# A one-core decoder layer: merge, second norm and down projection in other slots, and the low parts of the input projection's weights kept in DRAM between the halves

## The chip, the cores and the metric

The kernel runs on one core of a Trainium2 chip. The metric is the device time of one execution in microseconds, the median of several runs; lower is better.

## The reference

One layer of a hybrid decoder for a prompt of 1024 tokens and 8 decoding samples of one token each, with D = 1024. All arithmetic is fp32. Cut to what matters:

```python
h = _rms_norm(x, norm_mix_g)
proj = h @ w_in                                   # 1024 x 5888: 46 blocks of 128 columns
p_rwkv, p_hgrn, p_gate = split(proj)              # 14, 16 and 16 blocks
o_a = _rwkv7_mixer(p_rwkv, ...)                   # delta-rule matrix state, 8 heads of 64
o_b = _hgrn2_mixer(p_hgrn, ...)                   # gated linear recurrence, 4 heads of 128
gate_a, gate_b = split(sigmoid(p_gate))
merged = gate_a * (o_a @ w_up_a) + gate_b * (o_b @ w_up_b)
x = x + merged @ w_out                            # output projection
h = _rms_norm(x, norm_ffn_g)                      # the second norm
x = x + (silu(h @ w_ffn_gate) * (h @ w_ffn_up)) @ w_ffn_down
y = _rms_norm(x, norm_final_g)
```

The new states of both mixers, for the prompt and the samples, are outputs too.

## The kernel before

The tokens are worked in two halves, 512 tokens and then 512 tokens with the 8 samples (520 columns, in two chunks of 260). Activations lie transposed: channels on the 128 partitions, tokens along the columns. A half goes through these stages: input projection and mixers, merge (`push_merge`), output projection (`push_out`). The feed-forward network and the down projection then take both halves together.

Every product runs three times on TensorE, since operands are split: a high part (a copy rounded to the fast fp32r type) and a low part (the difference). `wload` does this for a weight block of 128 x 1024: SP loads the raw tile `w`, ACT copies it to `wh`, and GpSimd (POOL) subtracts, in four pieces, to make `wl`. Each of the three tags has two buffers. `mm3` then gives TensorE per block of 128 rows the products wh x high, wh x low and wl x high: 24 matmuls of 512 columns for a weight in the first half, 48 of 260 in the second.

Work is recorded by two streams. `parts` holds generators (norms, preparations and chains of the mixers); `stream` and `fillers` hold dense weights (`push`, `fill`). `drive` advances the part that is due by the recorder's own clock and puts a step of dense work (`dense_step`) wherever no part is due; when a weight is begun, the next one is loaded (`preload`). A scheduler then sets the final order on each engine, and each engine runs its queue in order. Nearly all DMAs are issued by SP, whose queue is in order as well: a DMA that waits holds all that stand behind it. The fillers are the gates' weights.

In the RWKV mixer (`rwkv_prep`) each of four pairs of heads inverts triangular blocks through bursts of small DMAs to DRAM and back (d1, nb, na, d2, t32, ubd, ebd, tbd); `rwkv_chain` is a chain of small matmuls, DVE and ACT steps.

Slots are fixed tiles by tag (h 16, t 6, p 11, w 19, d 4 of double width, a 2 of triple width; n and s in the second part). After the second half's merge the kernel splits all eight merged tiles in one go (in `push_out`, into slots of w, d and a), and the second norm of the first half (`first_second_norm`: a sum of squares, `rstd`, `spread`, and in `second_norm` the scaled tiles, their differences and splits for a fast product scheme, stored in `h2t[0]`) is driven while the merge's weights run:

```python
    start("norm", first_second_norm())
    drive()
    finish_stream()
    ...
    h2t[1] = push_out(1, merged, x1, residual)
```

After the output projection come two blocks of the feed-forward network for the first half alone (`push_plain`), beside which the second half's second norm runs, then the network in the fast scheme, then the down projection in four groups of acts (`gslots`, `load_acts`, `push_down`).

## Time and profile before

| | us |
|---|---|
| median of 3 runs | 1928.99 |
| lowest of the runs | 1925.67 |
| the profiled execution | 1921.57 |
| its span, first to last instruction | 1919.8 |
| PE busy | 1772.6 (92%) |
| DVE, POOL, ACT busy | 1078.6, 969.0, 808.7 |

The profiled execution is one run with the hardware profiler; its span leaves out 1.8 us around the first and last instruction. Its mean granted TensorE clock was 0.963 of full speed. Busy PE is not PE at its peak: at the lower clock the same matmul is busy for longer.

### The profile page before, as it was taken

The page shows a single profiled execution, that of the slowest core. Times are in us where ns is not written, and L with a number is a line of the kernel's source. Part 1 is how long each engine was busy: PE and PEld are TensorE (multiplying, and loading weights), DVE is VectorE, ACT ScalarE, POOL GpSimd, SP SyncE. Part 2 cuts the span into 40 slices and gives each one's busy share as a digit, 9 for nine tenths or more (in the row PEclk, how much of TensorE's full clock was granted, in tenths as well). Part 3 has the DMA queues.
Part 4 walks back from the last instruction along what each step waited for, and adds up shares of the span by engine and source line. Part 5 has one row for each costly group of instructions (what it writes and reads, how often), then busy time and mean ns, then how long its engine had stood idle before and what let it go on. Part 6 is the DMA issues. An engine that isn't in the chain of part 4 may idle for free. (4 is left out here: it accounts for less than half of the span.)

```text
span 1919.8 us, 32939 instructions
## 1 busy us (share of the span) xinstructions
PE 1772.6 (92%) x12376; PEld 1628.9 (85%) x12376; DVE 1078.6 (56%) x2315; ACT 808.7 (42%) x1601; POOL 969.0 (50%) x1131
## 2 busy tenths in 40 slices
PE   6998999988799799899889869999999999999997
PEld 5776778778678789788889769999999999889987
DVE  4476577657465366567554593856656665531214
ACT  4446556656342456354344453433333333421111
POOL 6545555645365456556364364654434343542342
PEclk9998999999899899889989889999999999999998
DMA  4233233343444225323434543123221322732212
GB/s 133 87 72 98 84 81 84 113 131 112 150 161 126 76 66 88 103 70 95 124 114 129 175 156 130 67 89 105 72 84 67 103 75 95 253 109 56 72 52 89
DMA packets 172304, 199.05 MB, mean 104 GB/s; under 512 B 99632, under 2 KB 108080, under 8 KB 172144
## 3 DMA queue, kind: packets, MB, share of 16 engines
q1 hardware_dynamic: 172144, 196.94, 34.3%
q8 instruction: 97, 1.59, 0.4%
q14 instruction: 63, 0.52, 0.1%
HBM read 156.30 MB, written 40.07 MB: 102 GB/s over the span
## 5 line engine op out<-in xcount | busy, mean ns | idle before, releaser
L160 ACT ACT_TABLE_LOAD x66 | 84.7, 1283 | 1.8 <-PEq L1825 0.7
L160 POOL TENSOR_TENSOR d__20102<-d__20102,d__20103 128x512 f32<-128x512 f32 (+1 forms) x14 | 14.2, 1016 | 21.3 <-ACT d__20103 L160 21.3
L160 DVE SCALAR_TENSOR_TENSOR w__6304<-p__6021,vec,pm__6305 128x512 f32<-128x512 f32 x1 | 0.7, 747 | 21.2 <-PE pm__6305 L238 21.2
L238 PE MATMUL pd__12144<-w__12090,wh__12128 128*128 128x260 f32 x1 | 0.6, 584 | 13.0 <-ACT w__12090 L160 13.0
L160 POOL TENSOR_TENSOR wl__1389<-w__1386,wh__1388 128x256 fp32r<-128x256 f32 x4 | 3.2, 841 | 17.0 <-ACT wh__1388 L160 17.0
L160 POOL COPY own<-wkv_st 64x64 f32<-64x64 f32 x16 | 6.2, 386 | 10.7 <-PE pm__4635 L238 3.3
L238 PEld LDWEIGHTS pd__12144<-w__12090,wh__12128 128*128 128x128 f32 x1 | 0.3, 288 | 13.2 <-ACT w__12090 L160 13.2
L160 POOL TENSOR_TENSOR wl__11476<-w__11473,wh__11475 128x256 fp32r<-128x256 f32 x4 | 3.7, 940 | 14.3 <-ACT wh__11475 L160 14.3
L238 PE MATMUL pm__219<-ones,t__196 128*128 128x1 f32 x4 | 1.0, 357 | 9.5 <-DVE t__196 L160 9.5
L160 POOL TENSOR_TENSOR wl__5125<-w__5122,wh__5124 128x256 fp32r<-128x256 f32 x4 | 3.6, 936 | 11.3 <-ACT wh__5124 L160 11.3
L160 POOL TENSOR_TENSOR wl__10054<-w__10051,wh__10053 128x256 fp32r<-128x256 f32 x4 | 2.8, 736 | 12.7 <-ACT wh__10053 L160 12.7
L160 POOL TENSOR_TENSOR wl__3944<-w__3941,wh__3943 128x256 fp32r<-128x256 f32 x4 | 3.3, 855 | 11.8 <-ACT wh__3943 L160 11.8
L238 PEld LDWEIGHTS pm__219<-ones,t__196 128*128 128x128 f32 x4 | 0.9, 322 | 9.5 <-DVE t__196 L160 9.5
L160 POOL TENSOR_TENSOR wl__12202<-w__12199,wh__12201 128x256 fp32r<-128x256 f32 x4 | 2.8, 734 | 11.2 <-ACT wh__12201 L160 11.2
L238 PE MATMUL pm__6333<-t__6313,ebd 128*128 128x128 f32 x8 | 2.1, 441 | 6.6 <-ACT t__6313 L160 6.6
L238 PEld LDWEIGHTS pm__6333<-t__6313,ebd 128*128 128x128 f32 x8 | 1.8, 328 | 6.8 <-ACT t__6313 L160 6.8
L238 PE MATMUL pm__5093<-w__4985,wh__5071 128*128 128x512 f32 x1 | 0.8, 792 | 7.3 <-ACT w__4985 L160 7.3
L160 POOL TENSOR_TENSOR wl__10209<-w__10206,wh__10208 128x256 fp32r<-128x256 f32 x4 | 2.8, 733 | 8.7 <-ACT wh__10208 L160 8.7
L160 POOL TENSOR_TENSOR wl__6274<-w__6271,wh__6273 128x256 fp32r<-128x256 f32 x4 | 2.8, 719 | 8.7 <-ACT wh__6273 L160 8.7
L160 POOL TENSOR_TENSOR wl__1106<-w__1103,wh__1105 128x256 fp32r<-128x256 f32 x4 | 5.1, 1291 | 4.0 <-ACT wh__1105 L160 4.0
L160 POOL TENSOR_TENSOR wl__11397<-w__11394,wh__11396 128x256 fp32r<-128x256 f32 x4 | 2.8, 732 | 7.9 <-ACT wh__11396 L160 7.9
L238 PE MATMUL pc__7693<-vsz__7629,kbt__7700 128*128 128x128 f32 x2 | 0.8, 500 | 6.4 <-ACT vsz__7629 L160 6.4
(23703 smaller groups left out, 8520.1 us busy)
## 6 DMA issues: line engine op xcount, KB each, us to landing
tbd<-t SPq DMA_DIRECT2D x32, 32.0 KB
w__166<-in_w_in SPq DMA_DIRECT2D x1, 512.0 KB
w__184<-in_w_in SPq DMA_DIRECT2D x1, 512.0 KB
w__452<-in_w_in SPq DMA_DIRECT2D x1, 512.0 KB
w__461<-in_w_in SPq DMA_DIRECT2D x1, 512.0 KB
w__501<-in_w_in SPq DMA_DIRECT2D x1, 512.0 KB
w__541<-in_w_in SPq DMA_DIRECT2D x1, 512.0 KB
w__581<-in_w_in SPq DMA_DIRECT2D x1, 512.0 KB
```

Of the source, the lines that this page charges most:

```text
L160: return f(*args, **kw)
L238: PE.matmul(out, lhsT, rhs, start=start, stop=stop)
```

## The change

Two things are changed.

First, in the first half each input-projection weight, when it begins, has its low part stored to DRAM (`store_low`, 44 blocks of 512 KB). The two blocks of the low-rank parts, worked at the very start, are not stored, so POOL subtracts for them in both halves. In the second half `wload_in` loads the raw block and the stored low part by two DMAs, ACT makes the high part, and POOL does nothing for it. Five of the second half's 46 input weights run at the end of the first half's mixers, ahead of the first merge; two of these are the low-rank ones.

Second, the second half's merged tiles are split one by one as each is done (`done` of `push_merge`), into the h slots; the second norm of the first half keeps its sum of squares beside the merge, but its scaling, differences and splits are driven beside the output projection and go to slots of w, d and a. The acts of the down projection take their slots in another order of tags.

```diff
@@ -255,7 +255,23 @@
     V.memset(ones, 1.0)
 
 
-    def wload(src, k=KD, dst=None):
+
+    lows, stores = {}, {}
+
+    def wload_in(m, half):
+        if half == 0:
+            w = wload(i["w_in"][m])
+            stores[id(w)] = m
+            return w
+        return wload(i["w_in"][m], low=lows.get(m))
+
+    def store_low(w):
+        m = stores.pop(id(w), None)
+        if m is not None:
+            lows[m] = dp.tile([P, KD, P], F32, tag="low", name=nm("low"), bufs=NIN)
+            SP.dma_start(out=lows[m], in_=w[1].bitcast(F32))
+
+    def wload(src, k=KD, dst=None, low=None):
         w = wp.tile([P, KD, P], F32, tag="w", name=nm("w"))[:, :k]
         SP.dma_start(out=w, in_=src)
         if dst is None:
@@ -263,7 +279,11 @@
             wl = wp.tile([P, KD, P], F32R, tag="wl", name=nm("wl"))[:, :k]
         else:
             wh, wl = dst
+        if low is not None:
+            SP.dma_start(out=wl.bitcast(F32), in_=low)
         A.activation(wh, w, AF.Copy)
+        if low is not None:
+            return wh, wl
 
         for a in range(0, k, PIECE):
             ks = slice(a, min(a + PIECE, k))
@@ -298,11 +318,11 @@
     spare = [SLOTS["p"]]
 
     def push(src, body, done=None, k=KD, need=0):
-        stream.append((lambda: wload(src, k), body, done, 1, need))
+        stream.append((src if callable(src) else lambda: wload(src, k), body, done, 1, need))
 
     def fill(src, body):
 
-        fillers.append((lambda: wload(src), body, None, 1, 0))
+        fillers.append((src, body, None, 1, 0))
 
     steps = [0]
 
@@ -319,6 +339,7 @@
                 return False
             w, body, done = loaded.pop(0)
             prepare(w, True)
+            store_low(w)
             current.append((body(w), done))
             steps[:] = [0, *PREPARE[isinstance(w, dict) and len(w["halves"]) == 2]]
             while len(loaded) < (stream[0][3] if stream else 1) and preload():
@@ -595,7 +616,7 @@
             elif m == 13:
                 A.activation(d, d, AF.Sigmoid)
 
-        return i["w_in"][m], body, done
+        return lambda: wload_in(m, half), body, done
 
     def loras(half, x, res):
         n = HLEN[half]
@@ -1063,7 +1084,7 @@
                 u[key] = y = slot(n_, tag=tag)
                 yield from product(w, x, half, lambda sl, ps: ev(y[:, sl], ps))
 
-            push(i["w_in"][col + hd], body, lambda: u["done"].add(key), need=tag == "p")
+            push(lambda: wload_in(col + hd, half), body, lambda: u["done"].add(key), need=tag == "p")
 
         for key, col, tag in (("fk", 18, "w"), ("q", 14, "p"), ("og", 26, "p"), ("iv", 22, "p")):
             item(key, col, tag, lambda y, ps: A.activation(y, ps, AF.Copy))
@@ -1262,13 +1283,13 @@
                 gates[m, b] = d = dp.tile([P, HLEN[half]], F32, tag="gate", name=nm("gate"), bufs=17)
                 SP.dma_start(out=d, in_=g)
 
-            fill(i["w_in"][30 + 8 * b + m], body)
+            fill(lambda: wload_in(30 + 8 * b + m, half), body)
 
         for m in range(KD):
             for b in range(2):
                 item(m, b)
 
-    def push_merge(m, half, src, gates, merged):
+    def push_merge(m, half, src, gates, merged, done=None):
         def body(w):
             y = merged[m]
             gs = [slot(HLEN[half], tag="t") for _ in range(2)]
@@ -1283,7 +1304,7 @@
                     V.tensor_tensor(g[:, sl], g[:, sl], ps, ALU.mult)
                 V.tensor_tensor(y[:, sl], gs[0][:, sl], gs[1][:, sl], ALU.add)
 
-        push(i["w_up"][m], body)
+        push(i["w_up"][m], body, done)
 
     def add_to(y):
         return lambda sl, ps: V.tensor_tensor(y[:, sl], y[:, sl], ps, ALU.add)
@@ -1361,7 +1382,9 @@
         mh, ml, rest = many(half, F32R)
         for m in range(KD):
             split(merged[m], mh[m], ml[m])
-
+        push_out_of(half, mh, ml, x1, done)
+
+    def push_out_of(half, mh, ml, x1, done=None):
         def item(m):
             push(
                 i["w_out"][m],
@@ -1371,7 +1394,6 @@
 
         for m in range(KD):
             item(m)
-        return mh + ml + rest
 
 
     xs = [slot(HP) for _ in range(KD)]
@@ -1382,7 +1404,9 @@
         for k in range(KD):
             SP.dma_start(out=xs[k][:, a:b], in_=i["xT"][k, :, a:b])
         src, body, _ = s["loras"][n]
-        gens.append(body(wload(src)))
+        w = src()
+        stores.pop(id(w))
+        gens.append(body(w))
         if n == 0:
             SP.dma_start(out=cst, in_=i["cst"])
     load_constants()
@@ -1444,8 +1468,9 @@
         pools[tag], bufs[tag], widths[tag] = fp, FSLOTS[tag], HP + NS
 
     merged = [slot(HLEN[1], tag="p") for _ in range(KD)]
+    mh, ml = h_slots(1)
     for m in range(KD):
-        push_merge(m, 1, src, s["gates"], merged)
+        push_merge(m, 1, src, s["gates"], merged, lambda m=m: split(merged[m], mh[m], ml[m]))
 
     x1 = [slot(HP, tag="p") for _ in range(3)]
     for _ in range(2):
@@ -1453,8 +1478,6 @@
     x1.append(slot(HP, tag="n"))
     for m in range(KD):
         SP.dma_start(out=x1[m], in_=x1d[m])
-    h2t = [[slot(HP, F32R, "h") for _ in range(16)] + [slot(HP, F32R, tag=y) for y in "w" * 11 + "n"], None]
-
     def operands(tiles, half):
 
         n = HLEN[half] // 2
@@ -1465,7 +1488,7 @@
         ops["B11"] = [[t[:, part * n : part * n + n] for t in tiles[6::7]] for part in range(2)]
         return ops
 
-    def second_norm(half, x1, acc, tiles):
+    def second_norm(half, x1, acc, tiles, b12=None):
         n = HLEN[half] // 2
         rs = rstd(acc, half)
         yield
@@ -1492,20 +1515,28 @@
             split(b1, h2, l2, G)
             yield
 
+    acc0 = slot(HP, tag="t")
+
+    def sums():
+        add = square_sum(acc0)
+        for k in range(KD):
+            add(x1[k])
+            yield
+
+    start("norm", sums())
+    drive()
+    finish_stream()
+
+    h2t = [[slot(HP, F32R) for _ in range(SLOTS["w"])], None]
+    for _ in range(2):
+        h2t[0] += parts_of(double(F32R), HP + NS)
+    for _ in range(2):
+        h2t[0] += parts_of(triple(F32R), HP + NS)
+    rest = h2t[0][7 * KD // 2 :]
+    h2t[0] = [y[:, :HP] for y in h2t[0][: 7 * KD // 2]]
     h2s = [operands(h2t[0], 0), None]
     b12 = [slot(HP, F32R, "s") for _ in range(KD // 2)]
-
-    def first_second_norm():
-        acc = slot(HP, tag="t")
-        add = square_sum(acc)
-        for k in range(KD):
-            add(x1[k])
-            yield
-        yield from second_norm(0, x1, acc, h2t[0])
-
-    start("norm", first_second_norm())
-    drive()
-    finish_stream()
+    x1_first = x1
     x1 = load_x(1, "pppppppp")
     x1e = dp.tile([KD, P, HLEN[1]], F32, tag="x1e", name="x1e", bufs=1)
     acc1 = slot(tag="n")
@@ -1516,10 +1547,13 @@
         for f, (a, b) in zip(add, CHUNKS[1]):
             f(x1[m][:, a:b])
 
-    h2t[1] = push_out(1, merged, x1, residual)
+    push_out_of(1, mh, ml, x1, residual)
+    start("norm", second_norm(0, x1_first, acc0, h2t[0], b12))
+    drive()
+    h2t[1] = mh + ml + rest
     for _ in range(2):
         h2t[1] += parts_of(double(F32R), HLEN[1])
-    h2t[1] += [slot(HLEN[1], F32R, "n") for _ in range(6)]
+    h2t[1] += [slot(HLEN[1], F32R, "n") for _ in range(7)]
 
 
 
@@ -1669,10 +1703,10 @@
                 yield from ts
 
     gslots = (
+        (("w", 16),),
+        (("h", 16), ("d", 8), ("n", 4)),
+        (("w", 19), ("a", 6), ("n", 3)),
         (("h", 16),),
-        (("n", 7), ("w", 13), ("d", 8)),
-        (("h", 16), ("w", 6), ("a", 6)),
-        (("w", 13), ("n", 3)),
     )
     x1s = [[slot(HP, tag="p") for _ in range(KD)], [slot(tag=y) for y in "pppttttt"]]
     f0s = [sum(FGROUPS[:g]) for g in range(len(FGROUPS))]
```

Where it moves instructions. On DVE, at the end of the second half's merge. The names: t and p tiles on the left of an addition are the merge's (p__11336 and p__11292 the last merged tile), rows of 128x520 are splits of merged tiles, and the others, on p, d, n and t tiles with 256 or 512 columns, are the second norm. Before:

```order
L160 TENSOR_TENSOR p__11336<-t__11974,t__11975 128x260
L160 TENSOR_TENSOR t__12055<-n__11342,t__12055 128x256
L160 TENSOR_TENSOR d__11340<-n__11342,d__11340 128x256
L160 TENSOR_TENSOR d__11340<-t__12055,n__11342 128x256
L160 TENSOR_TENSOR d__12098<-p__11333,d__12098 128x520
L160 TENSOR_TENSOR w__11373<-t__12055,w__11372 128x512
L160 TENSOR_TENSOR d__12099<-p__11334,d__12099 128x520
L160 TENSOR_TENSOR a__12100<-p__11335,a__12100 128x520
L160 TENSOR_TENSOR w__12091<-p__11329,w__12090 128x520
```

And now:

```order
L160 TENSOR_TENSOR t__11881<-t__11881,pd__11900 128x260
L160 TENSOR_TENSOR p__11292<-t__11880,t__11881 128x260
L160 TENSOR_TENSOR t__11880<-t__11880,pm__11915 128x260
L160 TENSOR_TENSOR t__11881<-t__11881,pd__11929 128x260
L160 TENSOR_SCALAR ms__11996<-pm__11991 128x4
L160 TENSOR_TENSOR p__11292<-t__11880,t__11881 128x260
L160 TENSOR_TENSOR h__11308<-p__11292,h__11300 128x520
L160 SCALAR_TENSOR_TENSOR p__11309<-p__11309,vec,pm__12027 128x512
L160 SCALAR_TENSOR_TENSOR d__11312<-d__11312,vec,pm__12027 128x512
L160 TENSOR_TENSOR w__11952<-p__11309,w__11952 128x256
L160 TENSOR_TENSOR s__11969<-p__11309,s__11969 128x256
```

Before, the norm's last operations stand among the merge's and the splits all stand behind them; now a tile's split follows its last addition, and the norm begins behind the last one.

On SP, in the first half's mixers, where one head pair's small copies go out (w are raw weights, low the stored parts, wl the low tiles in SBUF, ebd, t_105 and ubd pieces of the inverse). Before:

```order
L160 DMA w__1202<-in_w_in 128x1024
L160 DMA ebd<-d__855 32x4x32 x4
L160 DMA wa__2725<-in_wa 128x128
L160 DMA w__1270<-in_w_in 128x1024
L160 DMA t_105<-x__1121 16x4x16 x8
```

And now:

```order
L160 DMA w__1127<-in_w_in 128x1024
L160 DMA ebd<-d__871 32x4x32 x4
L160 DMA wa__2781<-in_wa 128x128
L160 DMA low__1125<-wl__1068 128x1024
L160 DMA low__1226<-wl__1130 128x1024
L160 DMA w__1228<-in_w_in 128x1024
L160 DMA w__1298<-in_w_in 128x1024
L160 DMA t_105<-x__1145 16x4x16 x8
```

The two stores stand ahead of the load of w__1228, which is w__1202 of before and stood ahead of ebd; the second store is that of the weight w__1127 loaded just above.

On SP, at the start of the second half's mixers. Before:

```order
L160 DMA w__6011<-in_w_in 128x1024
L160 DMA w__6093<-in_w_in 128x1024
L160 DMA ebd<-d__5766 32x4x32 x4
L160 DMA w__6169<-in_w_in 128x1024
L160 DMA vs__6495<-smp__6489 128x8x1
L160 DMA t_105<-x__6041 16x4x16 x8
L160 DMA ubd<-t_105 32x4x32 x4
L160 DMA t__6202<-t_105 128x4x32
L160 DMA tbd_97<-t_105 32x8x32 x4
L160 DMA w__6271<-in_w_in 128x1024
L160 DMA w__6379<-in_w_in 128x1024
```

And now, in two pieces of the same place:

```order
L160 DMA wl__6087<-low__715 128x1024
L160 DMA w__6163<-in_w_in 128x1024
L160 DMA w__6236<-in_w_in 128x1024
L160 DMA wl__6166<-low__777 128x1024
L160 DMA ebd<-d__5845 32x4x32
L160 DMA t_105<-x__6111 16x4x16 x8
L160 DMA wl__6239<-low__849 128x1024
L160 DMA ubd<-t_105 32x4x32
```

```order
L160 DMA w__6335<-in_w_in 128x1024
L160 DMA wl__6338<-low__918 128x1024
L160 DMA w__6448<-in_w_in 128x1024
L160 DMA tbd_97<-t__6420 32x4x32 x4
L160 DMA wl__6451<-low__982 128x1024
```

Each raw weight has now a fetch of its low part (wl<-low) near it, in the midst of the inverse's copies; w__6271 before is w__6335 now, and has its fetch behind it. A fetch writes a tile that two weights share in turn.

## Rows read from the trace of the kernel before

**Rows 1.** The page, part 1, busy us (share of span).

```profile
PE 1772.6 (92%) x12376; PEld 1628.9 (85%) x12376; DVE 1078.6 (56%) x2315; ACT 808.7 (42%) x1601; POOL 969.0 (50%) x1131
```

**Rows 2.** Busy time by stage, the columns in the first line.

```profile
core 0: us, PE busy (x) PEld busy (x) DVE busy (x) ACT busy (x) POOL busy (x), PEclk, DMA share, GB/s
40.00:475.00 435.00, 407.31 (x2274) 336.93 (x2273) 277.55 (x681) 243.00 (x500) 242.36 (x324) 0.98 0.35 98
605.00:1045.00 440.00, 388.80 (x3026) 369.98 (x3025) 254.47 (x657) 216.70 (x497) 239.32 (x299) 0.93 0.37 95
1110.00:1155.00 45.00, 29.38 (x222) 28.69 (x221) 41.87 (x69) 22.07 (x39) 29.30 (x29) 0.81 0.45 149
1150.00:1155.00 5.00, 5.00 (x28) 5.00 (x28) 2.64 (x5) 0.00 (x0) 0.00 (x0) 0.59 0.59 194
...
1245.00:1610.00 365.00, 365.00 (x3070) 365.00 (x3070) 225.49 (x377) 128.99 (x228) 164.91 (x117) 1.00 0.24 81
```

**Rows 3.** Waits of PE, 1110 to 1165 us (total, times, longest).

```profile
PE pd__12144 L238 <- ACT w__12090 L160: 13.0, 1, 13.0
```

**Rows 4.** Timeline at the merge's end, PE and DVE (start, us, instruction).

```profile
1133.40 0.28 PE L238 MATMUL pd__12023<-a__11298,wl__11887 128*128 128x260 f32 x1
...
1148.91 0.69 DVE L160 TENSOR_TENSOR w__12091<-p__11329,w__12090 128x520 fp32r<-128x520 f32 x1
```

**Rows 5.** Waits of PE, 605 to 1045 us, some of the largest.

```profile
PE pm__6333 L238 <- ACT t__6313 L160: 6.6, 1, 6.6
PE pc__7693 L238 <- ACT vsz__7629 L160: 6.4, 1, 6.4
PE pm__10091 L242 <- ACT w__9998 L160: 4.9, 1, 4.9
PE pm__6308 L242 <- DMA ubd<-t: 2.8, 1, 2.8
```

**Rows 6.** Timeline of PE, merge and restart: starts of matmuls.

```profile
1121.44 0.28 PE L238 MATMUL pm__11899<-w__11289,wh__11807 128*128 128x260 f32 x1
1121.56 0.28 PE L238 MATMUL pm__11899<-w__11290,wh__11807 128*128 128x260 f32 x1
...
1151.55 0.42 PE L238 MATMUL pd__12144<-w__12094,wh__12128 128*128 128x260 f32 x1
1151.77 0.42 PE L238 MATMUL pd__12170<-w__12093,wh__12128 128*128 128x260 f32 x1
```

**Rows 7.** Timeline of PE: the norm's two small steps.

```profile
1107.28 0.95 PE L238 MATMUL pm__11701<-ones,t__11383 128*128 128x1 f32 x8
...
1109.61 1.12 PE L238 MATMUL pm__11740<-cst,rs__11707 128*128 128x128 f32 x8
```

**Rows 8.** Timeline of POOL: one weight of the second half.

```profile
639.11 2.76 POOL L160 TENSOR_TENSOR wl__6274<-w__6271,wh__6273 128x256 fp32r<-128x256 f32 x4 [8.67 <-ACT wh__6273 L160]
```

**Rows 9.** Timeline of DVE and POOL, 1113 to 1116 us.

```profile
1113.25 1.57 POOL L160 TENSOR_TENSOR h__11356<-d__11340,h__11355 128x512 fp32r<-128x512 f32 x1 [0.53 <-ACT h__11355 L160]
...
1113.60 0.41 DVE L160 TENSOR_TENSOR t__11726<-t__11726,pd__11750 128x260 f32<-128x260 f32 x1
1113.94 1.17 DVE L160 TENSOR_TENSOR t__11759<-d__11340,t__11759 128x256 f32<-128x256 f32 x1
...
1115.71 0.41 DVE L160 TENSOR_TENSOR p__11337<-d__11340,p__11337 128x256 f32<-128x256 f32 x1
```

**Rows 10.** Timeline of SP (SPq) and ACT at the second half's start.

```profile
600.09 0.37 SPq L160 DMA_DIRECT2D w__5925<-in_w_in  x1
...
603.95 1.06 ACT L160 ACTIVATE wh__5927<-w__5925 128x1024 fp32r<-128x1024 f32 x1 [7.22 <-DMA w__5925<-in_w_in]
...
616.90 11.90 SPq L160 DMA_DIRECT2D t<-x__6041  x8
...
634.13 0.38 SPq L160 DMA_DIRECT2D w__6271<-in_w_in  x1
...
637.97 1.06 ACT L160 ACTIVATE wh__6273<-w__6271 128x1024 fp32r<-128x1024 f32 x1 [10.50 <-DMA w__6271<-in_w_in]
```

More of the change, by code (lines that the diff above doesn't have):

```diff
@@ L1493, in second_norm @@
             yield
-    h2s = [operands(h2t[0], 0), None]
-    b12 = [slot(HP, F32R, "s") for _ in range(KD // 2)]
-    def first_second_norm():
-        acc = slot(HP, tag="t")
-        add = square_sum(acc)
+    acc0 = slot(HP, tag="t")
+    def sums():
+        add = square_sum(acc0)
         for k in range(KD):
@@ L1503, in first_second_norm @@
             yield
-        yield from second_norm(0, x1, acc, h2t[0])
-    start("norm", first_second_norm())
+    start("norm", sums())
     drive()
     finish_stream()
+    h2t = [[slot(HP, F32R) for _ in range(SLOTS["w"])], None]
[5 more added lines that the diff above has]
+    h2t[0] = [y[:, :HP] for y in h2t[0][: 7 * KD // 2]]
+    h2s = [operands(h2t[0], 0), None]
+    b12 = [slot(HP, F32R, "s") for _ in range(KD // 2)]
+    x1_first = x1
     x1 = load_x(1, "pppppppp")
```

## The prediction

> **What bounds the kernel now.** I read the page's busy line first: PE is busy 92% of the span [rows 1], so only the 147 us in which it stands still, and the time it spends at the lower clock, can be won without less work. The table by stage [rows 2] says where these are. The feed-forward network and the down projection leave PE nothing to gain, for its busy time fills them. The second half's mixers (605 to 1045 us) have 51.2 us of idle PE (440 less 388.8) and a granted clock of 0.93; the end of their merge (1110 to 1155) has 15.6 us (45 less 29.4) and a clock of 0.81. The first half's mixers have 27.7 us.
>
> In the short stage the waits name one culprit: PE stood 13.0 us for the operands of the output projection [rows 3]. The reader is to see in DVE's order why: the split of the merged tiles (w__12091) starts at 1148.91, though the merge's last matmul was done at 1133.4 [rows 4]. DVE was never free in between: it is busy 41.9 of these 45 us [rows 2], with the second norm of the first half standing ahead of the splits. So there DVE bounds, not PE. In the mixers' stage the largest waits are on ACT, and for one DMA [rows 5]; none of the large ones is on POOL by name.
>
> **The change part by part.** *The second norm beside the output projection.* It removes the wait of 15.6 us. With it goes the slow restart: after the gap the matmuls of 260 columns start 0.22 us apart, where they start 0.12 us apart in the merge [rows 6], and the stretch from 1150 to 1155 was granted 0.59 [rows 2]: 28 matmuls there by 0.10 us is 3 us. Against that stand three small waits. The splits now follow each merged tile, so only the last of them is late: it needs a DVE product and sum, an ACT copy and a DVE subtraction, some 2.5 us, and PE reaches that operand after 21 matmuls of 0.12 us; 0 to 1 us, I take 1. The norm's two little PE steps have 8 matmuls (1.0 us) between them instead of 12; in the trace the second starts 2.3 us after the first, whose own 0.95 us is in that [rows 7], so about 1 us. And DVE now has the norm while it empties PSUM for the projection: of its 41.9 us I put some 12 to the merge and 6 to the splits, which leaves 24 for the norm; with 16 additions of 0.41 us and as many for the squares that is 37 us, under a projection of 8 x 48 x 0.12 = 46 us. It fits, but in bunches; PE has three dense PSUM buffers, so I take 2 us (0 to 12, the second if the norm is not done when the feed-forward network asks for it). Sum: 15.6 + 3 - 4 = **14 us won** (bounds 3 to 18). The other slots of the acts change no copy and no matmul; the down projection's groups load from tiles that come free no later, so 0.
>
> *POOL's subtractions.* For the 44 weights of the second half's input projection, four subtractions each are gone: 2.76 us by the row of one such weight [rows 8], and 41 of these weights lie in the mixers' stage, so 41 x 2.76 = 113 us of POOL's 239 there [rows 2]. None of this is on the path by itself: PE waits for others. What it can give is shorter queues and a faster DVE. The same DVE operation on 256 columns with both inputs in SBUF took 1.17 us while POOL subtracted and 0.41 us when POOL stood still; one with an input in PSUM took 0.41 us beside the same subtraction [rows 9]. The chain's own DVE steps read PSUM, so they gain only by a shorter queue ahead of them. Below: 0. Above: all waits of the stage but those for late DMAs. Three of its waits (2.8, 6.6 and 4.9 us) stand behind a late burst or a late weight, shown next, so 51.2 - 14.3 = 37 us. I take **8 us won**, near the lower end, because no large wait is on POOL. The GPSIMD Engine Reference of the Trainium skill (section Specifications) gives the same split: contention with DVE instructions that have two SBUF inputs. If that were the whole story, the chain's PSUM-reading steps would be unhelped and this term would stay near 0; by the rows' shorter queues it is 8.
>
> *The fetch of the low parts.* Each of the 44 adds an issue on SP and 512 KB. The price is the wait that comes with it: the fetch writes the tile that PE read two weights ago, so it stands on SP until PE has left that tile, and everything behind it on SP stands too: the next weights, the small copies of the triangular inverse, the samples' states. Before, that wait was POOL's. When PE starts weight n, the fetch for n+1 may go; 0.4 us to issue and, by a weight's own load, 600.09 to 603.95, 3.9 us to land [rows 10]. Weight n lasts 48 x 0.12 = 5.8 us at least, so there is 1.5 us of slack in a stretch with dense work alone, and more where the mixers' matmuls stand between. Where SP is late the slack is gone: eight copies of the inverse held SP 11.9 us, the next weight was issued at 634.13, and ACT stood 10.5 us for it, with PE behind it [rows 10]. Bounds: 0, and 48 us (second rival). I take **3 us lost**, since the new order has 10 to 48 other matmuls between most weights of the stage.
>
> Beside these rows the page DMA: Bandwidth & Descriptors of the Trainium skill (section Anatomy of one DMA) speaks against the change: a DMA engine never waits on a semaphore, the issuing sequencer does, before dispatch; that is the blocking just described. [...]
>
> *The store of the low parts in the first half.* 44 issues of some 0.4 us on SP and 23 MB of writing, at a DMA share of 0.35 [rows 2], which leaves room. The store waits for POOL's last subtraction. In most places the next load on SP waited for that same subtraction anyway, for it reuses the raw tile of the weight. In about eight places the order sets the store of weight n ahead of the load of n+1, which was a full weight earlier before; the chain of load, copy and first subtraction, 3.9 + 1.06 + 0.7 us, then starts after weight n is ready, whose 24 matmuls of 512 columns take over 5 us. 0 to 1.5 us each, so 0 to 12; I take **3 us lost**.
>
> **Sum.** 14 + 8 - 3 - 3 = 16 us. The profiled execution took 1921.6 us (span 1919.8), so 1905.6 us there. The median of the runs, 1929.0, lies 7.4 us above the profiled one; on that scale 1913 us. A measurement of this kernel tells about 2% from no change, which is 39 us: below 1890.4 or above 1967.6.
>
> **The rivals.** *The chain was held by POOL.* For it: DVE's operation is nearly three times as long under a subtraction [rows 9], and POOL stood 8.7 us at one weight with other work queued behind it [rows 8]. Against it: the named releasers [rows 5]. It takes the upper end, 37 us instead of 8: 1913 - 29 = 1884 us.
>
> *SP becomes the bound.* Four heads of the second half each send two long bursts of small copies. If each leaves a fetch late by the 10.4 us that 11.9 us of SP exceeds the 1.5 us of slack, but half of them meet mixer work that hides as much, then 8 x 6 = 48 us instead of 3: 1913 + 45 = 1958 us, slower than before. It decides wherever SP is held more than 1.5 us ahead of a fetch while dense work alone fills PE. For it: PE stood 9.4 us there already [rows 5, 10]. Against it: in the new order most raw weights are issued ahead of the fetch that waits.
>
> *The gap only moves.* DVE, at 37 of 46 us, falls behind and PE waits for PSUM or, at the start of the feed-forward network, for the norm's last tile: 3 us won instead of 14, so 1924 us. For it: DVE was full in the merge with the same norm. Against it: beside the norm the projection asks four operations a weight of DVE, where the merge asked six.
>
> **How the numbers follow.** Forecast 1913 us, 0.48; POOL held the chain, 0.20; SP the bound, 0.17; the gap moves, 0.15. The forecast's own range is 1900 to 1930. The upper rival at half its size is 1935, whole 1958, the lower one whole 1884; with the unknown ends of the fetches I set 1880 to 1950. Faster by over 2% takes some two thirds of the POOL case, 0.13; slower by over 2% a quarter of the SP case, 0.04; the rest, 0.83, is within.
>
> **What would show it.** In the new profile: the stretch after the merge with no PE wait over 2 us and a clock near 1.0; DVE busy under 46 us in the projection; POOL near 126 us in the second mixers and PE's idle time there about 45 us. Wrong would be: waits of PE on a low tile by DMA in the second half (SP the bound), idle time of 20 us or less there (POOL held the chain), or a wait of over 5 us at the feed-forward network's first weights (the gap moved).

## The result

| | median us | lowest |
|---|---|---|
| before, same chip | 1928.81 | 1925.67 |
| changed kernel | 1898.22 | 1891.34 |

The ratio on record is 0.9861, 95% interval [0.9837, 0.9885]: 27 us won, where 16 were forecast (the two medians of the table, of four executions each, are 30.6 us apart). The time lies in the range, and by 2% it counts as no change. On another chip the same kernel measured 0.9825 [0.9802, 0.9847], 34 us won (e5 below), so the gain is 27 to 34 us. The profiled execution of the changed kernel took 1904.76 us.

First its page, part 1, busy us; it answers [rows 1].

```profile
span 1902.9 us, 32863 instructions
...
PE 1780.1 (94%) x12376; PEld 1630.9 (86%) x12376; DVE 1052.5 (55%) x2315; ACT 812.0 (43%) x1603; POOL 832.0 (44%) x955
```

PE is idle 122.8 us instead of 147. Where they went is read from the table of busy time by stretches, as in [rows 2]: the first half's mixers, the second half's, its merge, and its output projection.

```profile
core 0: us, PE busy (x) PEld busy (x) DVE busy (x) ACT busy (x) POOL busy (x), PEclk, DMA share, GB/s
40.00:475.00 435.00, 404.30 (x2204) 331.63 (x2203) 268.73 (x664) 239.07 (x493) 234.68 (x315) 0.97 0.47 149
...
605.00:1045.00 440.00, 403.82 (x3155) 383.07 (x3153) 241.66 (x692) 225.16 (x507) 116.81 (x144) 0.93 0.58 149
...
1057.00:1123.00 66.00, 57.94 (x418) 55.07 (x418) 38.52 (x81) 29.86 (x48) 33.37 (x36) 0.90 0.51 172
1123.00:1176.00 53.00, 49.70 (x402) 49.11 (x401) 42.90 (x69) 24.36 (x46) 39.78 (x42) 0.97 0.47 156
```

In the second half's mixers PE is idle 36.2 us (440 less 403.8) against 51.2, with POOL at 117 us instead of 239. In the first half's mixers the idle time grew from 27.7 to 30.7 us, and the DMA share from 0.35 to 0.47. The wait of 13.0 us after the merge [rows 3] is gone. These are all the waits of PE in the output projection:

```profile
PE pd__12336 L238 <- DVE p__11977 L160: 1.9, 1, 1.9
PE pd__12283 L238 <- DVE p__11977 L160: 1.0, 1, 1.0
PE pm__12027 L238 <- POOL rs__11997 L160: 0.4, 1, 0.4
```

DVE's timeline shows why; it answers [rows 4]. The last merged tile's split starts 1.1 us after the start of its last addition, ahead of the norm, whose first scaling is the last line.

```profile
1123.38 0.42 DVE L160 TENSOR_TENSOR p__11292<-t__11880,t__11881 128x260 f32<-128x260 f32 x1
1124.51 0.70 DVE L160 TENSOR_TENSOR h__11308<-p__11292,h__11300 128x520 fp32r<-128x520 f32 x1 [0.71 <-ACT h__11300 L160]
1125.91 0.75 DVE L160 SCALAR_TENSOR_TENSOR p__11309<-p__11309,vec,pm__12027 128x512 f32<-128x512 f32 x1 [0.71 <-PE pm__12027 L238]
```

The largest waits of PE in the second mixers, which answer [rows 5], are of a new kind: two of them are for a fetched low tile, by DMA.

```profile
PE pc__7186 L238 <- ACT vsz__6887 L160: 8.1, 1, 8.1
PE pc__10188 L238 <- ACT vsz__10150 L160: 5.3, 2, 4.2
PE pd__6652 L238 <- ACT p__6454 L160: 4.4, 1, 4.4
PE pd__6652 L238 <- DMA wl__6578<-low__1063: 3.4, 1, 3.4
PE pd__7899 L238 <- DMA wl__7817<-low__2295: 3.2, 1, 3.2
```

The wait of 8.1 us names ACT, but behind it stands a raw weight. SP's timeline has its issue at 708.61, among fetches and small copies, and ACT's has the copy that waited for it; the copy then frees ACT for the step that PE wants. The weight took 13.5 us to land, where [rows 10] has 3.9. This belongs to the one execution and not to the order: in e5, the same kernel, it was issued at 709.54 and ACT began its copy at 717.31 without a wait for it, so it landed within 7.8 us.

```profile
708.61 0.46 SPq L160 DMA_DIRECT2D w__7234<-in_w_in  x1
709.17 0.38 SPq L160 DMA_DIRECT2D w__7348<-in_w_in  x1
...
714.06 0.34 SPq L160 DMA_DIRECT2D wl__7237<-low__1539  x1
```

```profile
722.15 1.06 ACT L160 ACTIVATE wh__7236<-w__7234 128x1024 fp32r<-128x1024 f32 x1 [5.67 <-DMA w__7234<-in_w_in]
```

This table has the stages of the profiled executions in us, worked out from PE's timelines: a merge, a projection, the network and the down projection from the first to the last matmul of their weights, the mixers what lies ahead of the merge. Gaps of 0.4 to 5.7 us that are equal in all kernels are left out. Executions far slower than the others are left out of the ratios and of this table: one of the kernel before (2442.92 us) and two of e11, its profiled one among them (2153.71 us, at a granted clock of 0.747).

```
                     mixers merge  out   mixers merge  gap   out   FFN  down
                     half 1             half 2
before                496.1  51.0  52.6  462.8  70.2  13.1  50.8  446.6  262.2
changed               501.9  55.0  52.7  446.3  65.7   0.8  52.6  448.1  265.7
e1  norm only         494.3  50.8  52.6  461.4  67.9   0.8  52.2  447.3  265.1
e2  low parts only    503.0  58.8  52.7  434.0  67.2  13.1  50.8  446.6  261.7
e3  no low parts      493.1  51.4  52.9  434.6  65.2   0.8  52.6  447.5  265.1
e4  DMAs on ACT       514.9  57.3  52.6  432.9  65.5   0.8  52.6  446.5  264.9
e5  changed again     496.2  58.2  52.7  440.8  65.3   0.8  52.6  446.7  265.1
e6  fetch only        501.5  49.1  52.6  434.8  64.2   0.8  52.2  445.9  266.0
e7  stores only       503.3  53.0  52.7  455.4  68.7   0.8  52.6  446.6  265.1
e8  stores on POOL    503.4  58.5  52.7  441.0  64.7   0.8  52.6  446.2  266.4
e9  half the blocks   503.3  50.9  52.7  434.5  67.4   0.8  52.2  445.2  265.1
e10 stores late       497.2  52.5  52.6  432.4  63.9   0.8  52.2  446.7  265.5
e12 memsets on POOL   497.9  52.3  52.6  430.1  72.7   0.8  52.6  446.8  265.0
```

From before to changed: 9.8 us lost in the first half, 16.5 won in the second mixers, 4.5 in the second merge, 12.3 in the gap; 1.8, 1.5 and 3.5 lost in the projection, the network and the down projection. That is 16.7 us between these two executions. One execution of each kernel was profiled, and the same kernel twice (changed, e5) differs by 5.7 us in the first mixers and by 5.5 in the second, so smaller differences of one stage show nothing by themselves.

### The profile page after: what moved, and what is told of

It is laid out like the page before. It is cut to its first block, busy times and chain, and to the rows that moved or that the text cites. A ratio compares the mean times of both kernels' runs of the same rounds, so it can differ in the third digit from the quotient of the medians.

```text
span 1902.9 us, 32863 instructions
## 1 busy us (share of the span) xinstructions
PE 1780.1 (94%) x12376; PEld 1630.9 (86%) x12376; DVE 1052.5 (55%) x2315; ACT 812.0 (43%) x1603; POOL 832.0 (44%) x955
## 2 busy tenths in 40 slices
DMA packets 184974, 245.18 MB, mean 129 GB/s; under 512 B 101040, under 2 KB 109488, under 8 KB 184816
## 5 line engine op out<-in xcount | busy, mean ns | idle before, releaser
L160 POOL TENSOR_TENSOR wl__1419<-w__1416,wh__1418 128x256 fp32r<-128x256 f32 x4 | 3.2, 843 | 16.0 <-ACT wh__1418 L160 16.0
L160 POOL TENSOR_TENSOR wl__11418<-w__11415,wh__11417 128x256 fp32r<-128x256 f32 x4 | 3.7, 944 | 14.6 <-ACT wh__11417 L160 14.6
L160 POOL TENSOR_TENSOR wl__5204<-w__5201,wh__5203 128x256 fp32r<-128x256 f32 x4 | 3.6, 930 | 11.8 <-ACT wh__5203 L160 11.8
L160 POOL TENSOR_TENSOR wl__1768<-w__1765,wh__1767 128x256 fp32r<-128x256 f32 x4 | 2.8, 737 | 13.1 <-ACT wh__1767 L160 13.1
L160 POOL TENSOR_TENSOR wl__4057<-w__4054,wh__4056 128x256 fp32r<-128x256 f32 x4 | 3.9, 1002 | 8.5 <-ACT wh__4056 L160 8.5
L160 POOL TENSOR_TENSOR wl__5151<-w__5148,wh__5150 128x256 fp32r<-128x256 f32 x4 | 3.2, 840 | 9.4 <-ACT wh__5150 L160 9.4
L160 POOL TENSOR_TENSOR wl__1068<-w__1065,wh__1067 128x256 fp32r<-128x256 f32 x4 | 4.4, 1130 | 6.2 <-ACT wh__1067 L160 6.2
L160 POOL TENSOR_TENSOR wl__11658<-w__11655,wh__11657 128x256 fp32r<-128x256 f32 x4 | 3.5, 892 | 7.5 <-DMA t__11814<-gate__10883 7.5
```

What stands on the lines that cost most here:

```text
L160: return f(*args, **kw)
```

## The experiments

Ratios are against the kernel before on the same chip, and differences in us are differences of ratios times its 1925 us. One ratio is uncertain by some 4 to 6 us.

**The two parts apart (e1, e2).** e1 has the norm, the splits and the slots, and neither stores nor fetches:

```diff
-        if half == 0:
-            w = wload(i["w_in"][m])
-            stores[id(w)] = m
-            return w
-        return wload(i["w_in"][m], low=lows.get(m))
+        return wload(i["w_in"][m])
```

> The second norm, the splits and the slots as in the change; low parts neither stored nor fetched, POOL subtracts in both halves as before. Theory A (two separate gains: the closed gap after the merge, and POOL's relief in the second half less what SP pays for it): the gap alone, 11 to 15 us won, so 1914 to 1917 us. Theory B (the low path nets nothing, and the whole gain of the change, 1.4% or 27 us, comes from the norm and the slots): 1900 to 1905 us.

Measured: 1911.14 us, ratio 0.9932 [0.9913, 0.9951], 13 us won. e2 is the kernel before with `store_low`, `wload_in` and the fetch in `wload`, and with the norm, the splits and the slots of before:

```diff
+        if low is not None:
+            SP.dma_start(out=wl.bitcast(F32), in_=low)
...
+            store_low(w)
```

> The kernel before with only the store and the fetch of the low parts; norm, splits and slots as before. Theory A: the rest of the gain, 12 to 16 us won, 1913 to 1917 us, with the wait of 13 us after the second half's merge still there. Theory B: within 4 us of the kernel before, 1925 to 1933 us.

Measured: 1899.46 us, ratio 0.9860 [0.9836, 0.9884], 27 us won. The norm does what was reckoned. The low parts give more than either theory had, and the rival, that they net nothing, is refuted. 13 and 27 make 40, more than the 27 to 34 of the whole change.

**Relief without its price (e3), and another queue (e4).** e3 stores and fetches nothing, and in the second half uses the high part again in place of the low part:

```diff
-            stores[id(w)] = m
...
-            SP.dma_start(out=wl.bitcast(F32), in_=low)
+            wl = wh
```

> The changed kernel without any store or fetch, and without subtraction in the second half for these 44 weights: the high part stands in for the low part there, so the second half's input projection loses its low weight parts. It has the same matmuls. Theory A: POOL's relief without its price: the 18 us of DVE waits that PE lost, and none of the 7 us of waits for fetches nor of the 6 to 10 us that the first half lost, so 1875 to 1890 us. Theory B: no more than the norm gives, 1898 us or above.

Measured: 1878.06 us, ratio 0.9747 [0.9725, 0.9769]. Against e1 that is 36 us, the worth of leaving the subtractions out with no DMA in their place, 29.5 of it in the second mixers (461.4 to 434.6 us) and merge by the profiled executions. e4 is the changed kernel with stores and fetches issued by ACT:

```diff
+    LQ = Clocked(nc.scalar, "SP")
...
-            SP.dma_start(out=lows[m], in_=w[1].bitcast(F32))
+            LQ.dma_start(out=lows[m], in_=w[1].bitcast(F32))
...
-            SP.dma_start(out=wl.bitcast(F32), in_=low)
+            LQ.dma_start(out=wl.bitcast(F32), in_=low)
```

> The changed kernel with the 88 stores and fetches issued by ACT instead of SP, so that a fetch that waits for PE no longer holds SP's queue. If SP's blocking is the price of the fetch (theory A): 4 to 12 us below the changed kernel, 1887 to 1894 us, unless ACT is now held instead, by the store that waits for POOL: then 1900 us or above. Theory B: no difference from the changed kernel, 1898 us.

Measured: 1900.01 us, ratio 0.9871 [0.9852, 0.9890], nothing won against the changed kernel. The second mixers are as short as without any DMA (432.9), but the first half's are 13 us longer still: ACT now stands for POOL's subtractions, in this wait of ACT for instance:

```profile
ACT t__887 L160 <- POOL wl__782 L160: 4.6, 1, 4.6
```

**The price apart (e5 to e8).** e5 is the changed kernel again, to have it beside the others.

> The changed kernel itself, beside the others. Theory A (the norm's gain of 13 us and the low parts' gain of 27 us, measured apart, add): 1925 - 40 = 1885 us, so 1880 to 1890. Rival (they don't add: the late weights of the fetch in the second mixers eat what the norm wins): 1895 to 1902 us again. In the profile the norm's gain, the 12 us after the second merge, must be there in both cases; the rival has second mixers of 445 us or more, theory A 434 to 440.

Measured: 1890.58 us, ratio 0.9825 [0.9802, 0.9847], between the two. e6 stores one low part and fetches that one 44 times:

```diff
-        return wload(i["w_in"][m], low=lows.get(m))
+        return wload(i["w_in"][m], low=None if m in (12, 13) else next(iter(lows.values())))
...
-        if m is not None:
+        if m is not None and not lows:
```

> One low part is stored and fetched for all 44 weights of the second half, so the low parts of 43 weights are another weight's; the 43 other stores are left out, the 44 fetches stay. Theory A (the store makes the first half 10 us longer, and half of that is lost in the end; the fetch costs the rest of the 20 us between the changed kernel and the one without any low parts): first half's mixers and merge back at 493 to 496 and 51 us, total 1886 to 1893. Rival (the first half's delay is absorbed by the wait for the inverse at the second half's start, the fetch alone has the price): 1895 to 1900. Were the fetch free: 1878.

Measured: 1881.00 us, ratio 0.9779 [0.9756, 0.9802], below theory A's range. Without the stores the changed kernel is 9 us faster than e5; the fetches have the 6 us to e3, which the two intervals don't tell from nothing. e7 keeps the stores and fetches nothing:

```diff
-        return wload(i["w_in"][m], low=lows.get(m))
+        return wload(i["w_in"][m])
```

> The stores stay, nothing is fetched, and POOL subtracts in the second half as before; the norm and the slots are as in the changed kernel. Without the stores this is the kernel of 1911 us. Theory A: the first half 10 us longer, of which half or more comes through to the end: 1916 to 1921 us. Rival (the second half's first wait for the inverse absorbs it): 1910 to 1914 us, with the first half 10 us longer and the second mixers 10 us shorter than in the kernel with the norm alone (461 us).

Measured: 1918.41 us, ratio 0.9974 [0.9956, 0.9992], 8 us above e1. So the stores cost 8 to 9 us by two comparisons. In the profiled executions the first half is 11.2 us longer than in e1 and the second mixers are 6 us shorter, which is near what the same kernel differs by. That the first waits of the second half absorb the delay, as the rival has it, is not shown: those for the inverse and for the step behind it, 1.5 and 6.8 us in e1, are 0.7 and 6.4 here. e8 issues the stores from POOL:

```diff
+    LQ = Clocked(nc.gpsimd, "SP")
...
-            SP.dma_start(out=lows[m], in_=w[1].bitcast(F32))
+            LQ.dma_start(out=lows[m], in_=w[1].bitcast(F32))
```

> The changed kernel with the stores issued by POOL, behind its own last subtraction of each weight; the fetches stay on SP. Theory A (the store's price is that it stands on SP until POOL is done and holds the next load): first half's mixers and merge at 494 to 498 and 51 to 53 us instead of 502 and 55, total 5 to 10 us under the changed kernel on this chip. Rival (the price is the 23 MB of writing, or the issue costs POOL as much): first half 502 us or more, total within 3 us of the changed kernel or above it.

Measured: 1893.89 us, ratio 0.9851 [0.9827, 0.9875], not better than e5. Each issue holds POOL 0.6 us, behind a stop of 0.3 us for its own subtraction in most places: the 44 issues take 26 us of POOL's time. The load of the place shown below goes out early again in e8, at 100.78, and still the first half is as long as with the stores on SP, so here POOL's time may be the price; no run takes it away. A row of POOL's timeline of e8:

```profile
81.08 0.57 POOL L160 DMA_DIRECT2D low__849<-wl__782  x1 [0.30 <-POOL wl__782 L160]
```

**How the stores cost (e10, e11).** The place is best seen in SP's timeline of e7. The load of the next weight, w__1065, stands behind the store of low__1063 and four small copies, and goes at 108.00:

```profile
105.05 0.43 SPq L160 DMA_DIRECT2D low__1063<-wl__987  x1
105.59 2.36 SPq L160 DMA_DIRECT2D t__1055<-d__1053  x4
108.00 0.46 SPq L160 DMA_DIRECT2D w__1065<-in_w_in  x1
```

The store's own subtraction, of wl__987, was done by 101.9. What SP stood for is DVE, for copies that are ahead of the store; these are POOL's row and SP's wait from 97 to 109 us in e7, and then the load of the same weight in e1, which goes ahead of those copies, at 96.42:

```profile
99.05 2.82 POOL L160 TENSOR_TENSOR wl__987<-w__984,wh__986 128x256 fp32r<-128x256 f32 x4 [2.05 <-ACT wh__986 L160]
SPq L160 <- DVE nb__895 L160: 5.6, 1, 5.6
```

```profile
96.42 0.35 SPq L160 DMA_DIRECT2D w__1043<-in_w_in  x1
```

In e7 ACT waits 4.62 us for that weight, and PE then 1.8 for ACT, as ACT's timeline and the waits of PE have it:

```profile
112.41 1.06 ACT L160 ACTIVATE wh__1067<-w__1065 128x1024 fp32r<-128x1024 f32 x1 [4.62 <-DMA w__1065<-in_w_in]
```

```profile
PE pd__1139 L238 <- ACT wh__1067 L160: 1.8, 1, 1.8
```

This is what DMA: Bandwidth & Descriptors of the Trainium skill (section Anatomy of one DMA) says, that the sequencer which issues a DMA waits for its semaphore, and the trace agrees: SP stood 5.6 us with w__1065 behind it, and once issued the weight was there within 4.4 us. Behind PE's wait, which ends at 113.5, the granted clock falls to the lower of its two levels, 1.2 GHz (0.50). The rows of PE from 115 to 120 us in e7 and then in e10, the next experiment, where PE has no such wait:

```profile
115.00:120.00 5.00, 5.00 (x22) 0.50 0.25 99
```

```profile
115.00:120.00 5.00, 5.00 (x27) 1.00 0.66 220
```

From 100 to 200 us the granted clock is 0.91 in e7 and 0.95 in e1. e10 records the store behind the next weight's load:

```diff
             prepare(w, True)
-            store_low(w)
             current.append((body(w), done))
...
             while len(loaded) < (stream[0][3] if stream else 1) and preload():
                 pass
+            store_low(w)
```

> The changed kernel with each store recorded behind the next weight's load instead of ahead of it; all stores and fetches stay. Theory A (the price of the stores is SP's order: a store that waits for POOL holds the next load, ACT then waits for the raw weight): the first half's mixers and merge back from 502 and 55 to 495 to 498 and 51 to 53 us, total 5 to 8 us under the changed kernel, 1883 to 1888. Rival (the price is the 23 MB of writing in the queue): first half and total as in the changed kernel, 1890 to 1898.

Measured: 1880.31 us, ratio 0.9771 [0.9743, 0.9799], below theory A's range and as fast as e6, which has a single store, though it moves the same 245.18 MB as the changed kernel. At the same place SP has the load first, at 105.26, and PE has no wait for ACT there; the clock from 100 to 200 us is back at 0.95:

```profile
105.26 0.43 SPq L160 DMA_DIRECT2D w__1063<-in_w_in  x1
105.81 2.35 SPq L160 DMA_DIRECT2D t__1055<-d__1053  x4
108.20 0.46 SPq L160 DMA_DIRECT2D low__1072<-wl__985  x1
```

```profile
100.00:200.00 100.00, 89.39 (x445) 0.95 0.46 133
```

e10 beats both kernels: by 2.3% the kernel before, and the changed one by 10 us (e5; the intervals just don't overlap). By the stage table the first half takes 554.4 to 561.8 us in the kernels with all stores ahead of the loads on SP (changed, e2, e5, e7), 544.5 to 550.2 in those without any store, and 549.7 in e10. So most of the stores' price is their place on SP and what the order then does to the loads, not their bytes. The other part of the profiled difference between e5 and e10 lies in the second mixers (440.8 and 432.4 us), which hold no store; it is not explained, and near what one kernel differs by there. e11 is e7 with an eighth of each store:

```diff
-            SP.dma_start(out=lows[m], in_=w[1].bitcast(F32))
+            SP.dma_start(out=lows[m][:, 0], in_=w[1][:, 0].bitcast(F32))
```

> The kernel with the stores alone (no fetches, POOL subtracts in both halves), but each store writes 64 KB instead of 512 KB, so that seven eighths of each low part are left out of the store; it waits for the same subtraction. Theory A (SP's order is the price): as with whole stores, 1916 to 1920 us, first half 503 and 53 us. Rival (the traffic is): as with the norm alone, 1909 to 1913 us, first half 494 and 51.

Measured: 1913.66 us, ratio 0.9940 [0.9917, 0.9963], near the norm alone. It looks like the rival, but it decides nothing: with the smaller store the scheduler also set loads ahead of DMAs that wait (at the place above, w__1065 now stands ahead of the copies that SP waits for, and the load after it ahead of the copies to t__1055), so two things changed at once.

**What POOL's rest is worth (e9, e12).** e9 stores and fetches the odd blocks only:

```diff
-            stores[id(w)] = m
+            stores[id(w)] = m if m % 2 else None
```

> The changed kernel, but only the odd-numbered blocks of the input projection are stored and fetched (22 of 44); POOL subtracts for the others in both halves. If relief and price both go with the number of blocks (35 us won by POOL's rest and 14 lost by stores and fetches for 44), the low path is worth half of its 21 us beyond the norm's 13: 1924 - 13 - 10 = 1901 us. Rival (the relief is saturated: once POOL is no longer full, more of it gives nothing, while the price halves): 1885 to 1891, as fast as the whole change or faster.

Measured: 1890.41 us, ratio 0.9826 [0.9796, 0.9856], the rival's number. In the profiled executions half the relief makes the second mixers as short (434.5 us) as all of it without DMAs (434.6). e12 gives POOL work back in e3, in place of the subtractions:

```diff
+            G.tensor_copy(wl[:, 0, 0:1].bitcast(F32), wh[:, 0, 0:1].bitcast(F32))
+            for _ in range(4):
+                G.memset(wl.bitcast(F32), 0.0)
+            return wh, wh
```

> As in the kernel without low parts in the second half (the high part stands in for the low part there, nothing is stored or fetched), but POOL gets work back in place of each weight's four subtractions: a copy of one column that waits for the high part, and four memsets of the whole 128x1024 low tile, which no matmul reads. Theory Q (the 36 us of POOL's rest come from its queue: small steps of the mixers no longer stand behind subtractions): the gain goes, 1900 to 1911 us with 450 to 461 us of second mixers, though DVE's 64x512 operations take their 0.69 us. Theory C (they come from DVE, whose operations on SBUF are slowed by the subtractions): 1876 to 1886 us with 434 to 440 us, if those DVE operations still take 0.69 us; if the memsets slow them to 0.8 us and more, C also says 1900 or above and the run doesn't tell them apart. Theory L (PE waited for late low parts): 1876 to 1882 in either case, since no matmul waits for POOL here.

Measured: 1884.07 us, ratio 0.9775 [0.9742, 0.9807]. POOL's queue is fuller than in the kernel before (287 us against 239 [rows 2]; the four memsets take 3.8 us, the subtractions 2.76 [rows 8]), and yet the second mixers are the shortest of all, 430.1 us (with the merge behind them 502.8, against 499.8 in e3 and 529.3 in e1). Its window and a row of POOL's groups:

```profile
605.00:1045.00 440.00, 406.95 (x3246) 387.53 (x3245) 249.77 (x692) 230.69 (x526) 287.05 (x355) 0.96 0.40 107
```

```profile
L160 POOL MEMSET wl__5932<- 128x1024 f32 x4 | 3.8, 954 | 0.1
```

Theory Q, the queue, is refuted. What the memsets don't do is slow DVE. Here is one pair of DVE's operations on 64x512 in SBUF in e1 (shortest, mean and longest in ns, first and last start), with the subtractions of POOL that the second of the pair ran beside, and then the same pair in the changed kernel:

```profile
L160 DVE TENSOR_TENSOR a__8987<-w__8481,w__8719 x2: 703/2052/3401, 855.8 to 856.5; 64x512 f32<-64x512 f32 x2
856.55 2.80 POOL L160 TENSOR_TENSOR wl__8933<-w__8930,wh__8932 128x256 fp32r<-128x256 f32 x4
```

```profile
L160 DVE TENSOR_TENSOR a__9005<-w__8572,w__8757 x2: 685/687/689, 861.5 to 862.2; 64x512 f32<-64x512 f32 x2
```

The first of e1's pair took 0.70 us, the second 3.40. e12 has both kinds of POOL's work in a row. DVE's operation on 64x512 takes 0.67 us beside a memset and 1.44 beside a product or sum of the mixers on POOL, which reads SBUF:

```profile
726.46 2.97 POOL L160 MEMSET wl__7446<- 128x1024 f32 x3
729.40 1.39 POOL L160 TENSOR_TENSOR w__6725<-w__6629 128x512 f32<-128x512 f32 x1
727.90 0.67 DVE L160 TENSOR_TENSOR d__7694<-w__7059,w__7060 64x512 f32<-64x512 f32 x1
729.91 1.44 DVE L160 TENSOR_TENSOR d__7694<-w__7059,w__7060 64x512 f32<-64x512 f32 x1
```

So the mixers' own work on POOL slows DVE too, with and without subtractions: in the nine pairs of this kind in the second half one operation takes 1.00 us in the mean in e1, 0.81 in e3, 0.78 in e12 and 0.70 in the changed kernel.

Over the whole run DVE is busy 1082.0 us in e1, 1056.6 in e3 and 1059.6 in e12, by part 1 of their pages:

```profile
PE 1773.1 (93%) x12376; PEld 1629.1 (85%) x12376; DVE 1082.0 (57%) x2315; ACT 809.8 (42%) x1601; POOL 970.7 (51%) x1131
```

```profile
PE 1768.0 (94%) x12376; PEld 1625.3 (87%) x12376; DVE 1056.6 (56%) x2315; ACT 810.4 (43%) x1603; POOL 838.5 (45%) x955
```

```profile
PE 1770.8 (94%) x12376; PEld 1626.9 (86%) x12376; DVE 1059.6 (56%) x2315; ACT 808.0 (43%) x1601; POOL 1008.4 (53%) x1175
```

The page SBUF — State Buffer of the Trainium skill (section Who interferes with whom) has the rule for it: a DVE instruction with two SBUF inputs contends with a GpSimd instruction that reads SBUF, not with one that only writes it. The trace agrees: memsets that fill POOL for 48 us more of the stage than before leave DVE 22 of the 25 us. That leaves theory L as well. Without a subtraction the weight is ready one step earlier and its raw tile is free after ACT's copy, in e12 as in e3. Sums of the waits over the second mixers speak for DVE. PE's waits for DVE take 24.1 us in e1, 12.4 in e9, 9.4 in e3 and 9.0 in e12; its waits for a low tile of POOL, which theory L has to shorten, are 0.5 us in e1. What is left for L is indirect: ACT stands 24.1 us for raw weights in e1 and 16.1 and 15.5 in e3 and e12, and PE's waits for ACT take 23.3, 16.9 and 20.6. Both gains come and go together in all these kernels, so how the 36 us divide between faster DVE and earlier weights is not shown by a run and stays open.

## Why the prediction was right, and where it was off

**The sum.** Forecast: 14 + 8 - 3 - 3 = 16 us won. By the experiments: 13 + 36 - 6 - 9 = 34, and 27 to 34 measured. That these add up to the 34 of e5 is no check: each is a step of one chain of kernels, from before over e1, e3 and e6 to e5, and in another order a step can measure otherwise (the norm's does, see what stays open). The time fell in the range and the sign was right, but the nearness of 16 to 27 is in part luck: of the 28 us by which POOL's term was too small, the 9 by which the two DMA terms were too small took a third back.

**The second norm (14 forecast, 13 measured).** Right, with the mechanism as put: no wait over 2 us after the merge, DVE busy 42.9 us in the projection (37 were reckoned, 46 was the limit), and the first weights of the feed-forward network wait for 2.5 us at most. The gap only moves: refuted. The items fit less well than the term. The 15.6 us are all the idle time of the stretch of 45 us; the wait in it was 13.0 [rows 3], and the gap shrank by 12.3. One item was wrong, that the acts' other slots cost nothing: the down projection is 3 us longer in every kernel that has them. In the changed kernel its waits are no longer in sum (2.8 us against 2.7 in its first 51 us), but there the clock was granted 0.90, where it was 1.00 before. In the same stretch it was 1.00 in e2, which has the old slots, and 0.93 in e1, e3, e5, e6, e10 and e12. The rows of before and of the changed kernel for these 51 us:

```profile
1649.00:1700.00 51.00, 48.24 (x302) 42.48 (x301) 24.36 (x40) 16.88 (x29) 29.04 (x27) 1.00 0.61 197
```

```profile
1631.00:1682.00 51.00, 48.07 (x269) 41.24 (x268) 19.50 (x32) 16.40 (x27) 25.33 (x26) 0.90 0.56 179
```

What moved the clock there, with nearly equal waits, wasn't tried. The shorter merge (2.3 us in e1), which the sum didn't have, pays most of it back; that is luck.

**POOL's subtractions (8 forecast, 36 measured).** This is the step that failed: "I take 8 us won, near the lower end, because no large wait is on POOL." The upper end, 37, was the one. A releaser's name tells which engine came last, not why it was late: without the subtractions PE's waits for DVE fell from 24.1 to 9.4 us and those for ACT from 23.3 to 16.9 (e1 to e3), though POOL had been named for 0.5. The sign that was set for it, idle time of 20 us or less, did not come (36.2 in the changed kernel, 45 had been expected with the forecast; POOL busy 117 us, 126 expected). The reason that was given for a gain, "a shorter queue ahead of them", is refuted by e12. The rule of the GPSIMD Engine Reference of the Trainium skill (section Specifications), contention with DVE instructions that have two SBUF inputs, was taken to leave the term near 0 because the chain reads PSUM. That was too narrow: other operations of the mixers have two SBUF inputs, such as a__8987 above. The rival "the chain was held by POOL" (1884 us) had the size, and without the DMAs' price the kernel would have been near it (e3, 1878).

**The fetches (3 forecast, about 6 measured).** The signs of the second rival are there, PE's waits for low tiles by DMA (3.4 and 3.2 us), but not its price of 48 us: with all 44 fetches the second mixers take 434.8 us in e6 and 434.6 without them. (The 48 was not what its own terms give: eight bursts of 10.4 us with half of them hidden are 42.) The 6 us are the difference of two ratios whose intervals overlap, so 3 is not refuted. The term took 3.9 us for a landing; in one execution it was 13.5, at a place where e5 had 7.8 at most.

**The stores (3 forecast, 8 to 9 measured).** The mechanism was right as to the place in the order, and e10 shows it by undoing it. At the place shown, though, the load was not late by the store's wait for POOL, as the term has it, but because behind the store it also came behind copies that wait 5.6 us for DVE. The size was off: a place costs the wait and then the matmuls at the lower clock behind it, which the 0 to 1.5 us each left out.

**What stays open.** The norm's gain beside the low parts: e2 and the whole change have nearly the same ratio (0.9860, and 0.9861 or 0.9825), so of the 13 us between 0 and 7 are left. Up to the second merge both have the same order on SP, and yet their second mixers took 434.0, 446.3 and 440.8 us in three executions, and in the longest of the three the one weight that took 13.5 us to land held PE 8.1 us. No run tells whether this is all of it.

## What to carry to other kernels

An engine that no wait names can still hold a kernel back through what its instructions do to another engine's speed; look at the duration of one operation with it and without it before pricing its relief at nothing. A DMA that waits for a result belongs behind the loads in its queue: recording 44 stores one place later was worth 10 us here, as much as leaving them out. When a relief has a price in traffic, try half of it: half the blocks gave as much as the whole (ratios 0.9826 and 0.9825).

## What was unexpected of the hardware

A DVE operation on two SBUF tiles took 3.40 us beside POOL's subtractions and 0.70 just ahead of them, while memsets that kept POOL busier cost DVE next to nothing (0.67 us for one such operation beside a memset). A 512 KB load landed in 13.5 us in one execution and within 7.8 in another of the same kernel, at the same place among fetches and small copies. And behind one wait of PE of 1.8 us the granted clock from 115 to 120 us was 0.50, the 1.2 GHz level, with 22 matmuls in the stretch, where it was 1.00 with 27 in the kernel without that wait.
